# Down projections: three of eight pairs with seven products in each of three chunks, their steps alternating with half pairs, and a sixth raw buffer

## The chip, the cores and the metric

The kernel runs on one core of one Trainium2 chip. The metric is the time of one execution on the device in microseconds (us): the median of three runs, 2199.27 us before the change (2198.91 to 2200.62). The profile is of one further execution. Engines are named as the profile names them: PE is TensorE, DVE VectorE, ACT ScalarE, POOL GpSimd, SP SyncE, whose queue issues nearly all loads.

## The reference

Two transformer layers over 256 tokens of width 2048: a chunked softmax attention in the first, a stick-breaking attention in the second, each beside an attention into 256 memory tokens, and in both layers an MLP with a squared ReLU. Cut to the part that the change touches:

```
D_MODEL = 2048; SEQ = 256; D_FF = 4 * D_MODEL

def sq_relu_mlp(h, g, w_in, w_out):
    return jnp.square(jax.nn.relu(rms_norm(h, g) @ w_in)) @ w_out

for layer in range(2):
    ...
    h = h + jnp.concatenate([y_main, y_mem], axis=-1) @ w_o[layer]
    h = h + sq_relu_mlp(h, norm_mlp[layer], w_mlp_in[layer], w_mlp_out[layer])
```

`w_out` (8192 x 2048) is the down projection.

## The kernel before

All weights are float32 in HBM. Each is read once, in units of 128 x 1024 numbers (512 KB), into one of five `raw` buffers, and split into two parts that TensorE multiplies at its faster rate: `hi`, a cast by ScalarE (four buffers), and `lo = raw - hi`, a subtraction by VectorE (five buffers). A product of two split numbers takes three matmuls: hi by hi, hi by lo, lo by hi. `stream` lists the units in the order of use; `weights()` (line 235 and the lines before it are the preparing functions) hands out the next prepared unit and keeps up to four prepared ahead (`AHEAD`, 3). TensorE's instructions are kept in program order; those of VectorE, ScalarE and SyncE are put in order by a scheduler when the program is built, and each of those engines then works strictly in that order. A buffer is handed on when its last reader is done.

The MLP (`mlp`) goes through `w_in` and `w_out` in four chunks of 2048 hidden features. In each chunk an up stage (512 matmuls in the first) makes the squared activations `hid`, split in the same way (lines 1059 to 1061); then the down stage adds their product with a quarter of `w_out`. For chunks 0 to 2 the down stage is two calls of `pair_group`, one for each n, that is for 1024 of the output's columns. It goes through eight pairs j. A pair is two blocks of 128 hidden features by 1024 columns, seen as a 2 x 2 by 2 x 2 product of blocks: rows are the two halves of 128 tokens, the inner index the two feature blocks, columns the two halves of 512. There are two ways to multiply a pair:

- Directly: 8 block products, in two half pairs, one for each column half ("1" and "2"). Each half pair is one unit with one load, one cast (line 231) and one split (line 232), and takes 12 matmuls of 512 columns.
- With 7 products (`Sevenfold`, the pairs named in `SEVEN`): sums of blocks are multiplied, as in Strassen's scheme. Both sides of the pair are loaded into two raw buffers, which stay in use through four steps. Step 0 splits the left side, step 1 one block of the right side (a half-size split), step 2 subtracts twice within the raw buffers and splits the right side (lines 204, 205), step 3 adds and subtracts once more and splits the left side (lines 207, 208). The casts are line 209, the splits line 210. TensorE has 6, 3, 6 and 6 matmuls for them, 21 instead of 24. The sums of the activations, `s12` and `s34`, are made by `finish` while the up stage runs (lines 1077 to 1083).

```
if seven.step == 1:
    src, hi4, lo4 = b22, hi4[:, 0], lo4[:, 0]
elif seven.step == 2:
    nc.vector.tensor_tensor(b22, b22, b12, op=ALU.subtract)
    nc.vector.tensor_tensor(b12, b12, b11, op=ALU.subtract)
elif seven.step == 3:
    nc.vector.tensor_tensor(b11, b22, b11, op=ALU.add)
    nc.vector.tensor_tensor(b21, b21, b11, op=ALU.subtract)
nc.scalar.copy(hi4, src)
nc.vector.tensor_tensor(lo4, src, hi4.bitcast(F32), op=ALU.subtract)
```

A group adds its products in eight PSUM banks: four for the output blocks 11, 21, 12 and 22, and p1, p5, p6, p7 for the products that belong to several blocks. When a bank has its last product it is added to a buffer in SBUF (`add`, line 1019 on VectorE; in chunk 0 most are plain copies by ScalarE, line 1017): nine additions per group in chunks 1 and 2, as p1 goes to two buffers. The product sums (`extra`) are merged into the output sums by six additions per n (`merged`, line 984) after chunk 2; the scheduler puts those of the first group into the second group of that chunk. Chunk 3 has no pairs with 7 products.

Before the change the pairs with 7 products are j = 0, 3, 6 in chunk 0 and j = 2, 6 in chunks 1 and 2. A pair's four steps follow one another, and the eight pairs follow in the order of j.

Of the kernel before, what the change touches and what calls it, by code (L numbers as in the profile page):

```python
# [42 lines left out]
WARM_UP = 10  # L43


SEVEN = [(0, 3, 6), (2, 6), (2, 6), ()]


class InOrder:
# [38 lines left out]
def trunk(  # L88
# [17 lines left out]
    nc = Engines(tc)  # L106

    const = ctx.enter_context(tc.tile_pool(name="const", bufs=1))
    raws = ctx.enter_context(tc.tile_pool(name="raws", bufs=5))
    his = ctx.enter_context(tc.tile_pool(name="his", bufs=4))  # L110
    los = ctx.enter_context(tc.tile_pool(name="los", bufs=5))
    acts = ctx.enter_context(tc.tile_pool(name="acts", bufs=2))
    grp = ctx.enter_context(tc.tile_pool(name="grp", bufs=13))
    wide = ctx.enter_context(tc.tile_pool(name="wide", bufs=6))
    nar = ctx.enter_context(tc.tile_pool(name="nar", bufs=6))
    tiny = ctx.enter_context(tc.tile_pool(name="tiny", bufs=4))
    ps_mm = ctx.enter_context(tc.tile_pool(name="ps_mm", bufs=4, space=PSUM))
# [386 lines left out]
    def spread(r, scale, name):  # L504

        ps = ps_y.tile([P, 512], F32, name="spread", tag="y")
        for m in range(2):
            dg = nar.tile([P, P], F32, name="dg", tag="nar")
            nc.vector.tensor_scalar_mul(dg[:], ident[:], r[:, 2 * m : 2 * m + 1])
            mm(ps[:, m * P : (m + 1) * P], neg_ones[:], dg[:], True, True)  # L510
        rb = nar.tile([P, T], F32, name=f"rb_{name}", tag="bias", bufs=4)
        nc.vector.tensor_scalar_mul(rb[:], ps[:, :T], -1.0)
        rbs = nar.tile([P, T], F32, name=f"rbs_{name}", tag="bias", bufs=4)
        nc.vector.tensor_scalar_mul(rbs[:], rb[:], scale)
        return rb, rbs

# [130 lines left out]
        yield from soft_tail(p, [(0, T), (T, 2 * T)], rs, vm, j, y, NH + j, None, lag)  # L647

    def band_head(qt, kt_, vt, j, head, y, ready, lag):
        bias = nar.tile([P, T], F32, name="bias", tag="bias", bufs=4)  # L650
# [41 lines left out]
    def stick_head(q, kt_, vt, j, head, y, lags):  # L692
# [16 lines left out]
            out=sp[:, :N], in0=z[:, :N], scalar=0.0, in1=e[:, :N], op0=ALU.max, op1=ALU.add  # L709
        )  # L710
        strict(sp[:, :N])
        sp_hi = wide.tile([P, 512], F32R, name="sp_hi", tag="wide_r", bufs=2)
        nc.scalar.copy(sp_hi[:, :N], sp[:, :N])
        sp_lo = wide.tile([P, 512], F32R, name="sp_lo", tag="wide_r", bufs=2)
        nc.vector.tensor_tensor(
            sp_lo[:, :N], sp[:, :N], sp_hi[:, :N].bitcast(F32), op=ALU.subtract
        )
# [52 lines left out]
    def mlp_stream(l):  # L770
        for c in range(NCH):
# [169 lines left out]
    def mlp(l, xg_, sq, h, done):  # L941
# [51 lines left out]
        def pair_group(c, n, hid, factors):  # L993
# [27 lines left out]
            def tokens(kt, m):  # L1021
                return [hid[:, kt, i * T + m * P : i * T + (m + 1) * P] for i in range(2)]

            def part(unit, k2):
                return [x[:, k2 * 512 : (k2 + 1) * 512] for x in unit]

            for j in range(KT // 2):
                if j in SEVEN[c]:
                    s = [[x[:, i * P : (i + 1) * P] for x in factors[j]] for i in range(4)]
                    w = weights()  # L1030
                    add("p1", tokens(2 * j, 0), part(w, 0))
                    add("11", tokens(2 * j + 1, 0), part(w, 1))
                    w = weights()
                    add("12", s[3], part(w, 0))
                    slot()
                    w = weights()
                    add("p5", s[0], part(w, 0))
                    add("p7", s[2], part(w, 1))
                    w = weights()
                    add("p6", s[1], part(w, 0))  # L1040
                    add("21", tokens(2 * j + 1, 1), part(w, 1))
                    slot()
                    continue
                for col in "12":
                    w = weights()
                    for m in range(2):
                        for k2 in range(2):
                            add(f"{m + 1}{col}", tokens(2 * j + k2, m), part(w, k2))
                    slot()

        began = clock["slot"]
        for c in range(NCH):
# [4 lines left out]
            def finish(f, hid=hid, squares=squares, factors=factors, c=c):  # L1057
# [6 lines left out]
                if f % 2 == 0 or f // 2 not in SEVEN[c]:  # L1064
                    return

                s12 = nar.tile([P, T], F32, name="s12", tag="bias", bufs=4)
                s34 = nar.tile([P, T], F32, name="s34", tag="bias", bufs=4)
# [268 lines left out]
```

## Time and profile before

| | |
|---|---|
| Median of three runs | 2199.27 us |
| Profiled execution | 2200.56 us |
| Its span, first to last instruction | 2198.8 us |
| TensorE busy | 2185.8 us (99%), 11192 matmuls |
| VectorE busy | 1492.7 us (68%) |
| ScalarE busy | 1133.5 us (52%) |
| GpSimd busy | 322.8 us (15%) |
| Granted TensorE clock | 1.000 |
| Loads | 414.64 MB, 189 GB/s in the mean |

The page gives shares over the whole span, and stages differ, so most rows in the prediction are of a view of one stretch. A view of windows gives for each stretch its length, then busy time and number of instructions of PE, PEld (TensorE's loads of the stationary operand), DVE, ACT and POOL, then the granted clock, the DMA engines' busy share and GB/s. A timeline row is start, length, engine, line, operation, tile written and tiles read, shapes and count. A row of the chain of waits is start, length and what the end waited for in that time. A group of instructions has its count, total busy time, mean length in ns, and the engine's idle time before it with what ended that. Matmul ends are modelled: a 512-column matmul is shown with 0.39 us whether the next has begun or not, so the pace is read from starts.

### The profile page before, as it was taken

The page shows a single profiled execution, that of the slowest core. Times are in us where ns is not written, and L with a number is a line of the kernel's source. Part 1 is how long each engine was busy: PE and PEld are TensorE (multiplying, and loading weights), DVE is VectorE, ACT ScalarE, POOL GpSimd, SP SyncE. Part 2 cuts the span into 40 slices and gives each one's busy share as a digit, 9 for nine tenths or more (in the row PEclk, how much of TensorE's full clock was granted, in tenths as well). Part 3 has the DMA queues.
Part 4 walks back from the last instruction along what each step waited for, and adds up shares of the span by engine and source line. Part 5 has one row for each costly group of instructions (what it writes and reads, how often), then busy time and mean ns, then how long its engine had stood idle before and what let it go on. Part 6 is the DMA issues. An engine that isn't in the chain of part 4 may idle for free.

```text
span 2198.8 us, 30008 instructions
## 1 busy us (share of the span) xinstructions
PE 2185.8 (99%) x11192; PEld 1866.1 (85%) x11192; DVE 1492.7 (68%) x1989; ACT 1133.5 (52%) x1570; POOL 322.8 (15%) x349
## 2 busy tenths in 40 slices
PE   9999999999999999999999999999999999999999
PEld 8888888888788888888888889888878888888888
DVE  7765555677767767876676556567776777688654
ACT  7655445554555445445445447555455544444543
POOL 0010112621001001001240112362100100100100
PEclk9999999999999999999999999999999999999999
DMA  8655666655666666665666654466566567666564
GB/s 307 198 176 161 179 178 192 193 190 163 194 208 190 183 211 184 190 204 191 195 187 190 188 188 134 135 188 193 166 183 224 178 183 218 187 189 200 190 198 139
DMA packets 213313, 414.64 MB, mean 189 GB/s; under 512 B 13232, under 2 KB 144304, under 8 KB 213168
## 3 DMA queue, kind: packets, MB, share of 16 engines
q1 hardware_dynamic: 212592, 410.63, 62.2%
q10 hardware_dynamic: 576, 2.10, 0.3%
q8 instruction: 88, 1.44, 0.3%
q14 instruction: 57, 0.47, 0.1%
HBM read 410.58 MB, written 2.10 MB: 188 GB/s over the span
## 4 chain that ended last, share of the span: by engine, by line
PE 93%; DVE 3%; DMA 2%; issue 1%; ACT 1%; SPq 0%; ACTq 0%; DVEq 0%
PE acc L59 88%; DMA raw<-in_w_down 2%; PE tp L59 1%; PE yp L59 1%; DVE lo L210 1%; PE accs L59 1%; PE s L59 1%; PE z L59 1%; DVE lo L232 1%; DMA raw<-in_w_mem 1%; ACT hi L209 0%; DVE raw L207 0%; DVE raw L205 0%; DVE raw L204 0%; DVE d L1019 0%
## 5 line engine op out<-in xcount | busy, mean ns | idle before, releaser
L158 DVE TENSOR_TENSOR lo<-raw,hi 128x1024 fp32r<-128x1024 f32 (+1 forms) x524 | 643.9, 1237 | 406.4 <-ACT hi L155 286.0
L155 ACT CAST hi<-raw 128x1024 fp32r<-128x1024 f32 (+1 forms) x524 | 546.4, 1045 | 425.4 <-PE acc L59 358.2
L59 PE MATMUL acc<-hi,hid 128*128 128x512 f32 x1704 | 534.4, 390 | 0.1
L59 PE MATMUL acc<-mlpx,hi 128*128 128x512 f32 x2048 | 472.8, 390 | 0.2
L59 PEld LDWEIGHTS acc<-mlpx,hi 128*128 128x128 f32 x2048 | 381.7, 188 | 79.4 <-issue 1.7
L59 PEld LDWEIGHTS acc<-hi,hid 128*128 128x128 f32 x1704 | 319.8, 188 | 68.0 <-issue 1.3
L59 PE MATMUL acc<-lo,hid 128*128 128x512 f32 x852 | 331.9, 390 | 0.2 <-DVE lo L232 0.2
L232 DVE TENSOR_TENSOR lo<-raw,hi 128x1024 fp32r<-128x1024 f32 x192 | 231.2, 1222 | 105.7 <-ACT hi L231 104.2
L231 ACT CAST hi<-raw 128x1024 fp32r<-128x1024 f32 x192 | 198.2, 1052 | 172.1 <-PE acc L59 91.7
L1061 POOL TENSOR_TENSOR hid<-upsq,hid 128x256 fp32r<-128x256 f32 x128 | 119.4, 942 | 1109.9 <-ACT hid L1060 1109.9
L59 PEld LDWEIGHTS acc<-mlpx,lo 128*128 128x128 f32 x2048 | 250.6, 192 | 2.8
L59 PE MATMUL acc<-mlpx,lo 128*128 128x256 f32 x2048 | 252.0, 283 | 0.0
L59 PE MATMUL acc<-hi,xg 128*128 128x512 f32 x640 | 210.5, 399 | 0.0
L209 ACT CAST hi<-raw 128x1024 fp32r<-128x1024 f32 x112 | 105.8, 946 | 164.0 <-DVE raw L205 60.5
L59 PEld LDWEIGHTS acc<-lo,hid 128*128 128x128 f32 x852 | 160.0, 188 | 34.2 <-DVE lo L232 1.3
L210 DVE TENSOR_TENSOR lo<-raw,hi 128x1024 fp32r<-128x1024 f32 x112 | 121.6, 1093 | 60.6 <-ACT hi L209 60.1
L59 PEld LDWEIGHTS acc<-hi,xg 128*128 128x128 f32 x640 | 120.2, 188 | 24.6
L433 ACT COPY low<-acc 128x256 f32<-128x256 f32 x188 | 69.0, 367 | 111.2 <-PE acc L59 111.2
L59 PE MATMUL acc<-lo,xg 128*128 128x512 f32 x320 | 124.7, 390 | 0.0
L59 PE MATMUL acc<-y,hi 128*128 128x512 f32 x512 | 119.9, 391 | 0.0
L59 PEld LDWEIGHTS acc<-y,hi 128*128 128x128 f32 x512 | 95.0, 188 | 19.1
L1060 ACT CAST hid<-upsq 128x256 fp32r<-128x256 f32 x128 | 51.8, 406 | 72.1 <-DVE upsq L1059 72.0
(195 smaller groups left out, 2266.8 us busy)
## 6 DMA issues: line engine op xcount, KB each, us to landing
raw<-in_w_up SPq DMA_DIRECT2D x256, 512.0 KB, 4.3
raw<-in_w_down SPq DMA_DIRECT2D x256, 512.0 KB, 6.0
raw<-in_w_in SPq DMA_DIRECT2D x80, 512.0 KB, 3.6
raw<-in_w_o SPq DMA_DIRECT2D x64, 512.0 KB, 3.8
raw<-in_w_mem SPq DMA_DIRECT2D x28, 512.0 KB, 5.2
raw<-in_w_kv_v SPq DMA_DIRECT2D x24, 512.0 KB, 3.6
raw<-in_w_kv_k SPq DMA_DIRECT2D x24, 512.0 KB, 4.3
raw<-in_w_q SPq DMA_DIRECT2D x24, 512.0 KB, 4.2
```

Of the source, the lines that this page charges most:

```text
L59: return self._tc.keep_in_program_order(fn(*args, **kwargs))
L155: nc.scalar.copy(hi[:, :n], raw[:, :n])
L158: nc.vector.tensor_tensor(lo, raw, hi.bitcast(F32), op=ALU.subtract)
L209: nc.scalar.copy(hi4, src)
L210: nc.vector.tensor_tensor(lo4, src, hi4.bitcast(F32), op=ALU.subtract)
L231: nc.scalar.copy(hi4, turned)
L232: nc.vector.tensor_tensor(lo4, turned, hi4.bitcast(F32), op=ALU.subtract)
L433: nc.scalar.copy(low[:], bank[:, T:])
L1060: nc.scalar.copy(hid[:, f, :T], a[:])
L1061: nc.gpsimd.tensor_tensor(hid[:, f, T:], a[:], hid[:, f, :T].bitcast(F32), op=ALU.subtract)
```

## The change

`SEVEN` names three pairs, j = 0, 2 and 4, in each of chunks 0 to 2. A new function `group_order` gives the order of work in a group: step 0 of a pair, then steps 1, 2 and 3, each with one half pair of the other five pairs behind it; the half pairs of column half 1 come first, then those of half 2; the last is left for the end. The stream of loads and `pair_group` both follow it. `raws` has six buffers for five and `wide` seven for six; the tags `wide_r` (two buffers) and `qb` (three) are gone: `sp_hi` and `sp_lo` now take `wide` buffers and the q tiles of the second layer `bias` buffers, of which there are five for four.

```
-SEVEN = [(0, 3, 6), (2, 6), (2, 6), ()]
+SEVEN = [(0, 2, 4), (0, 2, 4), (0, 2, 4), ()]
+
+def group_order(sevens):
+    others = [(j, col) for col in "12" for j in range(KT // 2) if j not in sevens]
+    steps = []
+    each = len(others) // (3 * len(sevens))
+    for j in sevens:
+        steps.append((j, 0))
+        for i in (1, 2, 3):
+            steps.append((j, i))
+            steps.extend(others[:each])
+            del others[:each]
+    return steps + others
...
-    raws = ctx.enter_context(tc.tile_pool(name="raws", bufs=5))
+    raws = ctx.enter_context(tc.tile_pool(name="raws", bufs=6))
...
-    wide = ctx.enter_context(tc.tile_pool(name="wide", bufs=6))
+    wide = ctx.enter_context(tc.tile_pool(name="wide", bufs=7))
...
-        sp_hi = wide.tile([P, 512], F32R, name="sp_hi", tag="wide_r", bufs=2)
+        sp_hi = wide.tile([P, 512], F32R, name="sp_hi", tag="wide")
...
-                    for j in range(KT // 2):
+                    for j, step in group_order(SEVEN[c]):
                         sides = [unit(2 * n + i, j) for i in range(2)]
-                        if j in SEVEN[c]:
-                            stream.extend([Sevenfold(*sides)] * 4)
-                        else:
-                            stream.extend(Gathered(ap) for ap in sides)
+                        if step == 0:
+                            seven = Sevenfold(*sides)
+                        stream.append(Gathered(sides["12".index(step)]) if step in ("1", "2") else seven)
...
-            for j in range(KT // 2):
-                if j in SEVEN[c]:
...
+            for j, step in group_order(SEVEN[c]):
+                w = weights()
+                if step in ("1", "2"):
+                    for m in range(2):
+                        for k2 in range(2):
+                            add(f"{m + 1}{step}", tokens(2 * j + k2, m), part(w, k2))
                     slot()
                     continue
...
+                s = [[x[:, i * P : (i + 1) * P] for x in factors[j]] for i in range(4)]
+                pairs = [
+                    (("p1", tokens(2 * j, 0)), ("11", tokens(2 * j + 1, 0))),
+                    (("12", s[3]),),
+                    (("p5", s[0]), ("p7", s[2])),
+                    (("p6", s[1]), ("21", tokens(2 * j + 1, 1))),
+                ][step]
+                for k2, (q, a) in enumerate(pairs):
+                    add(q, a, part(w, k2))
+                if step in (1, 3):
+                    slot()
...
-        q = nar.tile([P, T], F32, name=f"qb{hd}", tag="qb", bufs=3)
+        q = nar.tile([P, T], F32, name=f"qb{hd}", tag="bias", bufs=5)
```

Two places show how rows move. The first is VectorE in chunk 0 of layer 0, at the second pair with 7 products of the first group. `raw_0` and `raw_1` are the left and the right side of that pair; a `lo` from a plain `raw` is a half pair. Before:

```order
L232 TENSOR_TENSOR lo_4987<-raw_4985,hi_4986 128x1024
L210 TENSOR_TENSOR lo_5008<-raw_0_5003,hi_5007 128x1024
L210 TENSOR_TENSOR lo_5024<-raw_1_5005,hi_5023 128x512
L204 TENSOR_TENSOR raw_1_5005<-raw_1_5005 128x4x128
L205 TENSOR_TENSOR raw_1_5005<-raw_1_5005,raw_0_5003 128x4x128
L207 TENSOR_TENSOR raw_0_5003<-raw_1_5005,raw_0_5003 128x4x128
L208 TENSOR_TENSOR raw_0_5003<-raw_0_5003 128x4x128
L210 TENSOR_TENSOR lo_5040<-raw_1_5005,hi_5039 128x1024
L210 TENSOR_TENSOR lo_5058<-raw_0_5003,hi_5057 128x1024
L232 TENSOR_TENSOR lo_5071<-raw_5069,hi_5070 128x1024
```

And now (lines 221, 222, 224 and 225 are the old 204, 205, 207 and 208; 227 is the old 210 and 249 the old 232):

```order
L227 TENSOR_TENSOR lo_4996<-raw_0_4991,hi_4995 128x1024
L227 TENSOR_TENSOR lo_5012<-raw_1_4993,hi_5011 128x512
L221 TENSOR_TENSOR raw_1_4993<-raw_1_4993 128x4x128
L222 TENSOR_TENSOR raw_1_4993<-raw_1_4993,raw_0_4991 128x4x128
L249 TENSOR_TENSOR lo_5023<-raw_5021,hi_5022 128x1024
L224 TENSOR_TENSOR raw_0_4991<-raw_1_4993,raw_0_4991 128x4x128
L225 TENSOR_TENSOR raw_0_4991<-raw_0_4991 128x4x128
L227 TENSOR_TENSOR lo_5040<-raw_1_4993,hi_5039 128x1024
L249 TENSOR_TENSOR lo_5053<-raw_5051,hi_5052 128x1024
L227 TENSOR_TENSOR lo_5061<-raw_0_4991,hi_5060 128x1024
L249 TENSOR_TENSOR lo_5080<-raw_5078,hi_5079 128x1024
```

The splits of half pairs stand between the splits of the pair, and the four operations on the raw buffers are no longer in one piece.

The second place is VectorE in chunk 2 of layer 0, where the first group ends and the second begins. `d` and `e` are the sums in SBUF: rows that read `acc` empty a PSUM bank, rows of line 984 (now 1000) are the merges. Before, the second group opens with half pairs, and its first pair with 7 products comes later:

```order
L1019 TENSOR_TENSOR d_0_4025<-acc,d_0_4025 128x512
L1019 TENSOR_TENSOR d_2_4027<-acc,d_2_4027 128x512
L232 TENSOR_TENSOR lo_8353<-raw_8351,hi_8352 128x1024
L984 TENSOR_TENSOR d_0_4025<-d_0_4025,e_0_4029 128x512
L210 TENSOR_TENSOR lo_8374<-raw_0_8369,hi_8373 128x1024
L984 TENSOR_TENSOR d_0_4025<-d_0_4025,e_1_4030 128x512
L984 TENSOR_TENSOR e_0_4029<-e_0_4029,e_2_4031 128x512
L210 TENSOR_TENSOR lo_8390<-raw_1_8371,hi_8389 128x512
```

Now the second group opens with the steps of a pair:

```order
L227 TENSOR_TENSOR lo_8347<-raw_0_8342,hi_8346 128x1024
L1035 TENSOR_TENSOR d_2_4027<-acc,d_2_4027 128x512
L227 TENSOR_TENSOR lo_8359<-raw_1_8344,hi_8358 128x512
L221 TENSOR_TENSOR raw_1_8344<-raw_1_8344 128x4x128
L249 TENSOR_TENSOR lo_8376<-raw_8374,hi_8375 128x1024
L1035 TENSOR_TENSOR d_0_4025<-acc,d_0_4025 128x512
L222 TENSOR_TENSOR raw_1_8344<-raw_1_8344,raw_0_8342 128x4x128
L1035 TENSOR_TENSOR d_2_4027<-acc,d_2_4027 128x512
L1000 TENSOR_TENSOR d_0_4025<-d_0_4025,e_0_4029 128x512
L224 TENSOR_TENSOR raw_0_8342<-raw_1_8344,raw_0_8342 128x4x128
L227 TENSOR_TENSOR lo_8403<-raw_1_8344,hi_8402 128x1024
L1000 TENSOR_TENSOR d_0_4025<-d_0_4025,e_1_4030 128x512
```

Evacuations and merges now stand between the steps of a pair, where before they stood between half pairs for the greater part.

More of the change, by code (lines that the diff above doesn't have):

```diff
@@ L510, in spread @@
             mm(ps[:, m * P : (m + 1) * P], neg_ones[:], dg[:], True, True)
-        rb = nar.tile([P, T], F32, name=f"rb_{name}", tag="bias", bufs=4)
+        rb = nar.tile([P, T], F32, name=f"rb_{name}", tag="bias", bufs=5)
         nc.vector.tensor_scalar_mul(rb[:], ps[:, :T], -1.0)
-        rbs = nar.tile([P, T], F32, name=f"rbs_{name}", tag="bias", bufs=4)
+        rbs = nar.tile([P, T], F32, name=f"rbs_{name}", tag="bias", bufs=5)
         nc.vector.tensor_scalar_mul(rbs[:], rb[:], scale)
@@ L649, in band_head @@
     def band_head(qt, kt_, vt, j, head, y, ready, lag):
-        bias = nar.tile([P, T], F32, name="bias", tag="bias", bufs=4)
+        bias = nar.tile([P, T], F32, name="bias", tag="bias", bufs=5)
         nc.sync.dma_start(
@@ L711, in stick_head @@
         strict(sp[:, :N])
-        sp_hi = wide.tile([P, 512], F32R, name="sp_hi", tag="wide_r", bufs=2)
+        sp_hi = wide.tile([P, 512], F32R, name="sp_hi", tag="wide")
         nc.scalar.copy(sp_hi[:, :N], sp[:, :N])
-        sp_lo = wide.tile([P, 512], F32R, name="sp_lo", tag="wide_r", bufs=2)
+        sp_lo = wide.tile([P, 512], F32R, name="sp_lo", tag="wide")
         nc.vector.tensor_tensor(
@@ L1025, in part @@
                 return [x[:, k2 * 512 : (k2 + 1) * 512] for x in unit]
-            for j in range(KT // 2):
-                if j in SEVEN[c]:
[L1029 to L1041, printed above, removed]
+            for j, step in group_order(SEVEN[c]):
[4 more added lines that the diff above has]
+                            add(f"{m + 1}{step}", tokens(2 * j + k2, m), part(w, k2))
                     slot()
                     continue
[L1044 to L1048, printed above, removed]
+                s = [[x[:, i * P : (i + 1) * P] for x in factors[j]] for i in range(4)]
[8 more added lines that the diff above has]
+                if step in (1, 3):
                     slot()
@@ L1065, in finish @@
                     return
-                s12 = nar.tile([P, T], F32, name="s12", tag="bias", bufs=4)
-                s34 = nar.tile([P, T], F32, name="s34", tag="bias", bufs=4)
+                s12 = nar.tile([P, T], F32, name="s12", tag="bias", bufs=5)
+                s34 = nar.tile([P, T], F32, name="s34", tag="bias", bufs=5)
                 a11, a21 = squares[f - 1][:, :P], squares[f - 1][:, P:]
```

## The prediction

> **What bounds the kernel now.** I read the page first: the engines' busy time, the granted clock and the chain that ended last.
>
> ```profile
> span 2198.8 us, 30008 instructions
> PE 2185.8 (99%) x11192; PEld 1866.1 (85%) x11192; DVE 1492.7 (68%) x1989; ACT 1133.5 (52%) x1570; POOL 322.8 (15%) x349
> ...
> PEclk9999999999999999999999999999999999999999
> ...
> PE 93%; DVE 3%; DMA 2%; issue 1%; ACT 1%; SPq 0%; ACTq 0%; DVEq 0%
> PE acc L59 88%; DMA raw<-in_w_down 2%; PE tp L59 1%; PE yp L59 1%; DVE lo L210 1%; PE accs L59 1%; PE s L59 1%; PE z L59 1%; DVE lo L232 1%; DMA raw<-in_w_mem 1%; ACT hi L209 0%; DVE raw L207 0%; DVE raw L205 0%; DVE raw L204 0%; DVE d L1019 0%
> ```
>
> TensorE carries 93% of the chain at the full clock, so a matmul that is gone is time gone. The rest of the chain is mostly the loads of w_down and the split lines L204 to L210, the lines of a pair with 7 products. All six stretches that hold such pairs are inside the change. The view of windows, cut at the first matmul of each stretch and of the up stage behind it, gives their lengths (layer 0, chunks 0, 1, 2, then layer 1); the fourth pair of numbers is VectorE's busy time.
>
> ```profile
> 529.06:618.07 89.01, 85.73 (x367) 68.07 (x366) 68.91 (x75) 50.46 (x61) 3.08 (x2) 1.00 0.67 189
> 706.89:791.66 84.77, 84.75 (x373) 69.56 (x372) 66.35 (x76) 40.86 (x43) 2.69 (x2) 1.00 0.69 196
> 880.58:966.31 85.73, 85.06 (x373) 69.49 (x372) 69.33 (x82) 40.57 (x44) 2.69 (x2) 1.00 0.68 192
> 1578.31:1667.02 88.71, 85.34 (x367) 68.13 (x366) 68.82 (x75) 50.46 (x61) 3.08 (x2) 1.00 0.67 191
> 1755.87:1840.62 84.75, 84.73 (x373) 69.55 (x372) 66.39 (x76) 40.87 (x43) 2.69 (x2) 1.00 0.70 194
> 1929.59:2015.28 85.69, 85.04 (x373) 69.46 (x372) 69.36 (x82) 40.64 (x43) 2.69 (x2) 1.00 0.69 192
> sum 518.66, PE 510.64 PEld 414.27 DVE 409.17 ACT 263.86 POOL 16.91; mean PE 85.11 PEld 69.04 DVE 68.19 ACT 43.98 POOL 2.82
> ```
>
> TensorE's timeline inside the first stretch gives the unhindered pace:
>
> ```profile
> 561.24 0.61 PE L59 MATMUL acc<-hi,hid 128*128 128x512 f32 x2
> 561.70 0.39 PE L59 MATMUL acc<-lo,hid 128*128 128x512 f32 x1
> 561.92 0.61 PE L59 MATMUL acc<-hi,hid 128*128 128x512 f32 x2
> ```
>
> Three matmuls from 561.24 to 561.92 are 0.2267 us each (0.39 is the length of one, which overlaps the next). Chunk 0 has 366 of them and needs 82.97 us, chunks 1 and 2 have 372 and need 84.33. So TensorE stands still for 6.04 and 5.74 us in chunk 0, 0.44 and 0.42 in chunk 1, 1.40 and 1.36 in chunk 2: 15.4 us in all. Busy time hides part of this, since a matmul's length reaches over a gap of 0.16 us.
>
> The chain through chunk 0 says what these gaps are:
>
> ```profile
> 534.86 8.89 DMA raw<-in_w_down
> 543.86 0.63 ACT hi L209
> ...
> 545.24 0.70 DVE raw L204
> ...
> 547.42 0.69 DVE raw L208
> 548.11 1.15 DVE lo L210
> ...
> 549.30 15.75 PE acc L59 x68
> ```
>
> A load of a right half took 8.89 us, then a cast and six VectorE operations in a row, the four subtractions and additions L204 to L208 between two splits, held TensorE back until 549.30. Why was the load so late? The DMA queue's own timeline answers, and its own waits in this chunk:
>
> ```profile
> 531.72 0.37 SPq L227 DMA_DIRECT2D raw<-in_w_down  x1
> 533.39 1.84 SPq L192 DMA_DIRECT2D raw<-in_w_down  x2
> 536.34 3.00 SPq L227 DMA_DIRECT2D raw<-in_w_down  x3
> ```
> ```profile
> SPq L227 <- DVE lo L210: 18.0, 4, 6.2
> ```
>
> Six loads leave in a clump within 8 us; then the queue waits for the split of a pair, which holds two of five raw buffers through all four steps. Loads in a clump share the 16 DMA engines, and the pair's VectorE work falls on 4.8 us of TensorE work (21 x 0.2267).
>
> **The change part by part.**
>
> *Matmuls.* There were 3, 2 and 2 pairs with 7 products in the three chunks, times two column groups and two layers: 28. Now there are 3 x 3 x 4 = 36. Each of the 8 new ones has 21 matmuls in place of 24. 8 x 3 x 0.2267 = 5.4 us off, on the path. The Trainium skill (TensorE: Matmul & The Clock Gate, Back-to-back issue gap) gives about 131 ns per matmul for a sustained stream at N=512; by that the 24 would be worth 3.1 us. The timeline above has 0.2267 in this very stage, and I keep 5.4.
>
> *VectorE's work.* The groups give the price of a pair and of a half pair:
>
> ```profile
> L232 DVE TENSOR_TENSOR lo<-raw,hi 128x1024 fp32r<-128x1024 f32 x192 | 231.2, 1222 | 105.7 <-ACT hi L231 104.2
> L210 DVE TENSOR_TENSOR lo<-raw,hi 128x1024 fp32r<-128x1024 f32 x112 | 121.6, 1093 | 60.6 <-ACT hi L209 60.1
> L231 ACT CAST hi<-raw 128x1024 fp32r<-128x1024 f32 x192 | 198.2, 1052 | 172.1 <-PE acc L59 91.7
> L208 DVE TENSOR_TENSOR raw<-raw 128x512 f32<-128x512 f32 x28 | 19.4, 692 | 0.9
> L715 DVE TENSOR_TENSOR sp_lo<-sp,sp_hi 128x384 fp32r<-128x384 f32 x12 | 6.6, 554 | 1.1 <-ACT sp_hi L713 1.1
> ```
>
> A pair costs 4 x 1.09 + 4 x 0.69 = 7.1 us (L204, L205 and L207 are the same operation as L208), two half pairs 2.4: 4.7 more per added pair, 9.3 per chunk. VectorE's busy time rises to 66.35 + 9.3 = 75.7 us in chunk 1 and 78.6 in chunk 2, of 82.97 us that TensorE needs: 91 and 95%. That is cover, but thin, so I work out the tightest place.
>
> *The alternation.* One period is now: step 0, step 1, half pair, step 2, half pair, step 3, half pair, with 6, 3, 12, 6, 12, 6, 12 matmuls: 12.9 us. Spacing of back-to-back VectorE work, from its timeline:
>
> ```profile
> 927.38 1.22 DVE L210 TENSOR_TENSOR lo<-raw,hi 128x1024 fp32r<-128x1024 f32 x1
> 928.51 0.68 DVE L984 TENSOR_TENSOR d<-d,e 128x512 f32<-128x512 f32 x1
> 929.11 0.69 DVE L984 TENSOR_TENSOR e<-e,e 128x512 f32<-128x512 f32 x1
> ```
>
> 1.13 and 0.60 us. A period needs 6 x 1.13 + 5 x 0.60 = 9.8 us: 76%. Four `hi` buffers let a cast start when the unit four places ahead is done; three units then run, 21 matmuls or 4.8 us at least (step 0, step 1, half pair), against 1.05 + 1.22 = 2.3 us for a cast and a split. Lead 2.5 us. Before, the three were steps 1 to 3, 15 matmuls or 3.4 us, with four extra subtractions (2.4 us) in the way: that is the gap at 549.30, and it goes. Late next is the end of a group in chunks 1 and 2, where nine evacuations (L1019, 128x512 as L984) come in the last eight units: these are 6 + 3 + 12 + 6 + 12 + 6 + 12 + 12 = 69 matmuls, 15.6 us, against eight splits (7 x 1.13 + 0.60), four subtractions (2.4) and nine evacuations (5.4), 16.3 us. The 0.7 us over lies inside the lead. In chunk 2 six merge additions (L984, 3.6 us) follow in the next period, whose room is 12.9 - 9.8 = 3.1: 1.2 us over in all, and the rows of the order put one split behind five of these. Both ends: 0 if the lead covers it, 1.2 if not; I take 0.4 per layer, since the lead is twice the overrun but is shared with the casts.
>
> *Loads.* With six buffers a half pair's load leaves when an earlier half pair, or the right side, is split, one at a time. The nearest need is the half pair behind step 1: its buffer comes free at step 2 of the pair ahead, and units of 6 + 3 + 12 + 6 + 12 + 6 = 45 matmuls (10.2 us) pass before its cast; the split itself takes 2.3 of that. 7.9 us are left. The loads of such weights land so:
>
> ```profile
> DMA to landing us min/median/max: 3.7/6.8/10.4
> ```
> ```profile
> raw<-in_w_down SPq DMA_DIRECT2D x256, 512.0 KB, 6.0
> ```
>
> (the tile raw in chunk 2 of layer 0, and the page's median over the program). Spread out they should be near the 3.7; at worst one is 10.4 - 7.9 = 2.5 us late, which is the size of the lead. The Trainium skill (SBUF — State Buffer, The DMA setup-cost knee) puts a transfer at about 2 us plus bytes over 436 GB/s, an estimate of 3.2 us for 512 KB; by it no load would be late with five buffers either, the sixth would be worth nothing and all 15.4 us would belong to VectorE. The 8.89 us above speaks against that. In bytes nothing is new: 16 loads per group as in chunk 0, where the windows show 189 GB/s and a DMA share of 0.67.
>
> *Work with one answer.* The third pair's factors (s12, s34) are made in the up stages of chunks 1 and 2. VectorE's timeline has one set, and the chain has TensorE without a break from the start of chunk 2's up stage on:
>
> ```profile
> 872.51 1.46 DVE L1077 TENSOR_TENSOR s<-upsq 128x128 f32<-128x128 f32 x2
> ...
> 874.64 0.76 DVE L1083 TENSOR_TENSOR s_lo<-s,s_hi 128x256 fp32r<-128x256 f32 x2
> ```
> ```profile
> 18.03 2.79 PE accs L59 x11
> ...
> 48.06 8.16 PE acc L59 x36
> ...
> 791.68 121.73 PE acc L59 x656
> ```
>
> Four more sets of 2.9 us are hidden there (11.6 us if they were not): nothing. The sixth buffer also lets loads leave earlier elsewhere. At the start one load goes ahead of loads of mem and of bias; TensorE has every row of the chain from 18.03 to 56.22, so the cost is between one load's 3.7 us and a small gain, taken as 0. The re-tagged buffers (wide, bias) leave the order in the stick-breaking stage as it was but for one sp_lo. If the shared ring made each of the 12 heads wait for one L715, it would be 12 x 0.55 = 6.6 us; taken as 0, for the ring grew by one and the q tiles keep the three places that rb and rbs leave of five.
>
> *Sum.* Gaps left: 0.4 us in each of chunks 0 and 1, as chunk 1 has now, and 0.8 in chunk 2 (0.4 and the merges' 0.4), twice: 3.2 us. Off: 15.4 - 3.2 + 5.4 = 17.6 us. The profiled execution took 2200.56 us (span 2198.8 and 1.76 around it): 2183.0. The median of the runs, 2199.27, is 1.3 below that execution: 2181.7.
>
> **The rivals.**
>
> *Three pairs cost everywhere what they cost in chunk 0.* If the gaps come from the pairs' number and not from their clumping, every chunk stands still 5.9 us: 6 x 5.9 = 35.3 against 15.4, less 5.4: 14.5 slower, 2213.8. It decides from 20.8 us of gaps in all, 3.5 per chunk. For it: the two-pair chunks have gaps of 0.4 to 1.4, the three-pair ones 6; VectorE goes to 95%. Against: the chain lays these gaps on a late load and a clump of subtractions, and both are taken apart.
>
> *VectorE is late at each group's end.* An in-order engine that waits for an evacuation's last matmul has splits queued behind it, and TensorE waits for these. If no lead is left, the overrun is paid in full: 0.7 us at each of the eight group ends of chunks 1 and 2, and the merges' 3.6 us once per layer: 5.6 + 7.2 = 12.8, less the 0.8 counted above. 2181.7 + 12.0 = 2193.7. For: it is the one place over 100%. Against: the order puts a split between most evacuations.
>
> *Loads stay late in half of the places.* Chunk 0 keeps half of its 6.04 + 5.74 = 11.8 us, 5.1 more than counted: 2186.8. For: landing times up to 10.4 us. Against: the spread issue.
>
> **How the numbers follow.** A measurement of this kernel can tell 0.2%, 4.4 us, from no change. The forecast has 0.70, the loads 0.12 (both faster), VectorE at the group ends 0.10 (half of it within 0.2%), the first rival 0.08. Faster 0.87, same 0.05, slower 0.08. The low end is all gaps gone: 2199.27 - 20.8 = 2178.5. The high end takes in the late loads and some of VectorE's case: 2190. Left out is the first rival, and most of VectorE's: 0.18 at most.
>
> **What would show it.** In the changed profile the six stretches should be 83.4 to 84 us long, 366 matmuls each; VectorE 75 to 79 us busy in chunks 1 and 2, 69 in chunk 0; the DMA queue should issue no six loads in 8 us, and w_down's loads should be near 4 to 5 us in the median (6.0 on the page now); the chain should lose most of its 2% of w_down. Wrong would be: stretches over 86 us, TensorE waiting for L227 behind an evacuation line, or new time in the stick-breaking stage.

## The result

The changed kernel takes 2180.0 us (median of four runs, 2179.85 to 2180.22) against 2199.25 us of the kernel before (2198.91 to 2200.62): ratio 0.9911, 95% interval 0.9894 to 0.9929. The forecast was 2181.7, with a range of 2178.5 to 2190.

The page of the changed kernel, its lines on the engines, the clock and the chain that ended last; line 76 is now the matmul, L225 to L227 are what L208 to L210 were, and L249 is what L232 was:

```profile
span 2178.1 us, 30022 instructions
PE 2172.7 (100%) x11168; PEld 1863.8 (86%) x11168; DVE 1535.5 (70%) x2061; ACT 1151.1 (53%) x1594; POOL 324.3 (15%) x349
...
PEclk9999999999999999999999999999999999999999
...
PE 99%; DVE 1%; ACT 0%; issue 0%; ACTq 0%
PE acc L76 94%; PE tp L76 1%; PE accs L76 1%; PE yp L76 1%; PE s L76 1%; PE z L76 1%; DVE lo L249 0%; PE cold L76 0%; DVE d L1000 0%; DVE d L1035 0%; ACT hi L248 0%; DVE raw L225 0%; DVE raw L224 0%; DVE e L1000 0%; DVE raw L222 0%
```

TensorE's share of the chain rises from 93 to 99%; the loads of w_down, 2% before, are gone from it. There are 24 matmuls fewer and 72 VectorE instructions more. The six stretches, cut as before (length, TensorE, weight loads, VectorE, ...):

```profile
528.34:611.27 82.93, 82.93 (x367) 68.69 (x366) 69.53 (x75) 50.35 (x60) 2.80 (x2) 1.00 0.73 211
700.10:783.10 83.00, 83.00 (x368) 68.70 (x367) 75.79 (x88) 44.50 (x47) 2.81 (x2) 1.00 0.72 209
871.90:955.60 83.70, 83.28 (x367) 68.62 (x366) 78.80 (x94) 44.27 (x47) 2.81 (x2) 1.00 0.70 207
1567.50:1650.40 82.90, 82.90 (x367) 68.69 (x366) 69.50 (x75) 50.35 (x60) 2.81 (x2) 1.00 0.74 211
1739.30:1822.20 82.90, 82.90 (x367) 68.69 (x366) 75.70 (x88) 44.51 (x47) 2.80 (x2) 1.00 0.73 210
1911.10:1994.70 83.60, 83.18 (x367) 68.59 (x366) 78.71 (x94) 44.29 (x47) 2.81 (x2) 1.00 0.72 207
sum 499.03, PE 498.19 PEld 412.00 DVE 448.03 ACT 278.27 POOL 16.83; mean PE 83.03 PEld 68.67 DVE 74.67 ACT 46.38 POOL 2.80
```

Each needs 366 x 0.2267 = 82.97 us. Chunks 0 and 1 take that and nothing more; chunk 2 has 0.7 us over. The six lost 518.66 - 499.03 = 19.6 us of the 20.7 by which the span shrank; the rest is 0.7 us at the start and 0.1 us in each of four up stages behind them. (The medians differ by 19.3, as the profiled execution of before was 1.3 us above its median and that of the changed kernel, 2179.85, was not.)

The chain around the boundary of chunk 2's groups shows the one gap that is left:

```profile
903.81 7.04 PE acc L76 x31
...
910.87 1.06 ACT hi L248
...
911.96 1.23 DVE lo L249
913.19 0.60 DVE d L1035
913.79 0.60 DVE raw L222
914.39 0.60 DVE d L1035
914.99 0.60 DVE d L1000
...
919.13 1.15 DVE lo L249
...
920.32 1.90 PE acc L76 x7
```

Between the splits of two half pairs VectorE has evacuations (L1035), subtractions of a pair, one split of that pair and merge additions (L1000), without a break. The chain runs through them for 9 us until the second half pair's split lets TensorE go on at 920.32: the lead has been used up.

### The profile page after: what moved, and what is told of

Same layout as the page of the kernel before. It is cut to its first block, busy times and chain, and to the rows that moved or that the text cites. A ratio compares the mean times of both kernels' runs of the same rounds, so it can differ in the third digit from the quotient of the medians.

```text
span 2178.1 us, 30022 instructions
## 1 busy us (share of the span) xinstructions
PE 2172.7 (100%) x11168; PEld 1863.8 (86%) x11168; DVE 1535.5 (70%) x2061; ACT 1151.1 (53%) x1594; POOL 324.3 (15%) x349
## 4 chain that ended last, share of the span: by engine, by line
PE 99%; DVE 1%; ACT 0%; issue 0%; ACTq 0%
PE acc L76 94%; PE tp L76 1%; PE accs L76 1%; PE yp L76 1%; PE s L76 1%; PE z L76 1%; DVE lo L249 0%; PE cold L76 0%; DVE d L1000 0%; DVE d L1035 0%; ACT hi L248 0%; DVE raw L225 0%; DVE raw L224 0%; DVE e L1000 0%; DVE raw L222 0%
## 5 line engine op out<-in xcount | busy, mean ns | idle before, releaser
L175 DVE TENSOR_TENSOR lo<-raw,hi 128x1024 fp32r<-128x1024 f32 (+1 forms) x524 | 644.6, 1237 | 391.4 <-ACT hi L172 260.4
L172 ACT CAST hi<-raw 128x1024 fp32r<-128x1024 f32 (+1 forms) x524 | 546.7, 1045 | 413.7 <-PE acc L76 350.5
L76 PE MATMUL acc<-hi,hid 128*128 128x512 f32 x1624 | 521.6, 390 | 0.0
L76 PEld LDWEIGHTS acc<-hi,hid 128*128 128x128 f32 x1624 | 304.9, 188 | 63.0
L76 PE MATMUL acc<-lo,hid 128*128 128x512 f32 x812 | 316.2, 389 | 0.8 <-DVE lo L249 0.8
L248 ACT CAST hi<-raw 128x1024 fp32r<-128x1024 f32 x176 | 185.6, 1054 | 157.8 <-PE acc L76 111.9
L249 DVE TENSOR_TENSOR lo<-raw,hi 128x1024 fp32r<-128x1024 f32 x176 | 215.0, 1221 | 74.0 <-ACT hi L248 71.5
L226 ACT CAST hi<-raw 128x1024 fp32r<-128x1024 f32 (+1 forms) x144 | 136.2, 946 | 147.0 <-PE acc L76 95.1
L227 DVE TENSOR_TENSOR lo<-raw,hi 128x1024 fp32r<-128x1024 f32 (+1 forms) x144 | 159.4, 1110 | 45.6 <-ACT hi L226 44.3
L76 PEld LDWEIGHTS acc<-lo,hid 128*128 128x128 f32 x812 | 152.5, 188 | 33.1 <-DVE lo L249 1.7
```

Source lines behind the costliest of these rows:

```text
L76: return self._tc.keep_in_program_order(fn(*args, **kwargs))
L172: nc.scalar.copy(hi[:, :n], raw[:, :n])
L175: nc.vector.tensor_tensor(lo, raw, hi.bitcast(F32), op=ALU.subtract)
L248: nc.scalar.copy(hi4, turned)
L249: nc.vector.tensor_tensor(lo4, turned, hi4.bitcast(F32), op=ALU.subtract)
```

## The experiments

The first group takes the change apart: the order (the four steps in a row, or alternating), the counts (3, 2, 2 or 3, 3, 3) and the number of raw buffers. All start from the changed kernel, so that the re-tagged buffers are the same. "Gaps" is what the six stretches take beyond their matmuls at 0.2267 us. Where a total of gaps is given, a stretch goes from its own first matmul to the first one behind it; cut so, the kernel before has 15.6 us of gaps and the changed kernel 1.5.

**Five raw buffers.**

```
-    raws = ctx.enter_context(tc.tile_pool(name="raws", bufs=6))
+    raws = ctx.enter_context(tc.tile_pool(name="raws", bufs=5))
```

> The changed kernel with five raw buffers in place of six: alternation and three pairs stay. With five, a pair's left side takes the place of the left side before it, free only at step 3, and one half pair (12 matmuls, 2.7 us) lies between that split and the cast that needs the load; a load takes 3.7 to 10 us. Theory A (both parts are needed, the sixth buffer for the loads): loads of pairs come 1 to 3 us late, the lead of 2.5 us takes most of it, some 0.3 us is left for each of 36 pairs: 2190 (2184 to 2200), TensorE gaps of 1 to 4 us in each of the six stretches. Theory B (the clump of VectorE's subtractions was the whole cause, the sixth buffer is worth nothing beyond the start): 2180.7, gaps as with six.

Measured: 2191.83 us (2189.74 to 2195.16), ratio to before 0.9964 (0.9951 to 0.9977). The windows of chunk 2 in layer 0, then chunks 0 and 2 in layer 1, and the chain through the last of them:

```profile
875.00:961.10 86.10, 84.26 (x368) 68.42 (x368) 78.87 (x94) 43.91 (x47) 2.81 (x2) 1.00 0.71 201
1572.90:1655.90 83.00, 83.00 (x368) 68.74 (x367) 69.13 (x75) 50.37 (x60) 2.81 (x2) 1.00 0.76 211
...
1917.70:2006.80 89.10, 85.20 (x368) 68.14 (x367) 78.93 (x94) 44.04 (x47) 2.81 (x2) 1.00 0.70 194
```
```profile
1951.33 8.94 DMA raw<-in_w_down
1960.36 1.06 ACT hi L248
1961.44 1.23 DVE lo L249
...
1969.78 5.89 DMA raw<-in_w_down
```

With three pairs in every chunk the buffer decides: loads of 8.94 and 5.89 us stand in the chain again. The time is that of theory A, its picture is not: the 12.7 us of gaps are not spread over the pairs, one chunk 0 has none and the last chunk 2 has 6.

**The old order and counts, six buffers.** `group_order` gives a pair's four steps in a row and the pairs in the order of j, and `SEVEN` is that of before:

```
+    for j in range(KT // 2):
+        steps.extend([(j, i) for i in range(4)] if j in sevens else [(j, "1"), (j, "2")])
```

> The changed kernel's buffers (six raw ones and the new tags) with the order and the counts of before: four steps of a pair in a row, 3, 2 and 2 pairs. Theory A (both parts are needed): the loads' share of the 15.4 us of gaps goes, VectorE's clump stays: about half, 2191 (2188 to 2195). Theory B (VectorE's clump is all): 2198.5, gaps of 5 to 6 us in chunk 0 as before, only the start's 0.7 us gone. Theory C (late loads are all, the sixth buffer is the cure): 2184, gaps gone but for 1.4 us.

Measured: 2192.02 us (2191.70 to 2192.72), ratio 0.9964 (0.9950 to 0.9979). Chunks 0 and 1 of layer 0, and the chain through chunk 0 (the line of the matmul is L70 here, L218 to L221 the last additions and the split of a pair):

```profile
528.30:613.20 84.90, 83.99 (x367) 68.39 (x367) 69.23 (x75) 50.66 (x61) 3.33 (x2) 1.00 0.71 198
702.00:786.70 84.70, 84.68 (x373) 69.58 (x371) 66.37 (x76) 40.89 (x43) 2.68 (x2) 1.00 0.71 195
```
```profile
529.14 0.49 DVE raw L219
...
529.75 1.23 DVE lo L221
...
531.02 1.65 PE acc L70 x6
```

The gaps of chunk 0 fall from 5.9 to 1.9 us, and no load is left in its chain; the 0.4 and 1.4 us of chunks 1 and 2 stay as they were. So the buffer alone takes 8.1 of the 15.6 us away. Of the 7.5 that are left, some 5.6 are waits for a pair's split by VectorE; 1.8 lie at the group ends of chunks 1 and 2, where the trace shows no engine that TensorE waits for. Theories B and C both fall. That 8 us go with the buffer doesn't make them the loads' own: alternation takes them away without it, as the run with the old counts and five buffers shows below.

**Three pairs in every chunk in the old order, six buffers.** Only `group_order` is undone.

> The changed kernel with the order of before: three pairs in every chunk and six raw buffers stay, the four steps of a pair stand in a row again. Theory A: 5.4 us of matmuls and 0.7 us at the start off, and each of the six stretches has the half of chunk 0's 5.9 us that the buffer doesn't cure: 2193.2 + 18 - 15.4 = 2196 (2190 to 2202). Theory B (VectorE's clump is all): 6 x 5.9 = 35 us of gaps, 2213. Theory C (the sixth buffer is the cure, the order does nothing): 2180.

Measured: 2196.70 us (2196.03 to 2198.04), ratio 0.9983 (0.9974 to 0.9993): 1.4, 2.9 and 4.5 us of gaps in chunks 0, 1 and 2 (means of the two layers), 17.7 in all. The total is theory A's, but the gaps grow with VectorE's load from chunk to chunk, where it had put 3 us in each. Beside the sixth buffer, alternation is worth 17.7 - 1.5 = 16 us with three pairs.

**Three pairs in the old order, five buffers.** As the last, with five raw buffers: the first rival of the prediction, made real.

> Three pairs in every chunk with the order of before and five raw buffers: the counts of the changed kernel without alternation and without the sixth buffer. Theory A (late loads and VectorE's clump add up, and both are what alternation and the sixth buffer take away): the 5.9 us of chunk 0 before in every stretch, and in chunks 1 and 2 also the 1.5 and 3.1 us that they had over chunk 0 with six buffers: 6 x 5.9 + 2 x 4.6 = 44.6 us of gaps, 2199.3 + 44.6 - 15.4 - 5.4 = 2223 (2213 to 2230). The first rival of the prediction (as many pairs, as many gaps) gives 2213.8. Theory C (the pairs' number does not matter once their clumps are short): as old_order_three, 2197.

Measured: 2217.86 us (2217.57 to 2219.34), ratio 1.0077 (1.0061 to 1.0092). Layer 0 (chunks 0, 1, 2):

```profile
529.20:616.00 86.80, 86.00 (x368) 67.88 (x367) 69.42 (x75) 50.57 (x61) 2.54 (x2) 1.00 0.75 204
704.80:794.90 90.10, 86.09 (x368) 68.06 (x367) 76.35 (x88) 44.34 (x48) 2.55 (x2) 1.00 0.73 196
883.60:975.80 92.20, 86.99 (x368) 67.85 (x367) 79.65 (x94) 44.06 (x48) 2.54 (x2) 1.00 0.70 194
```

38 us of gaps, where the rival had 35.3: the counts alone make the kernel slower. Its total was nearly right, in part by luck, for it had put 5.9 us in every stretch and they are 3.8 in chunk 0, 6 to 7 in chunk 1 and 8 to 9 in chunk 2. What it lacked was that alternation and the buffer take the cause away.

**Alternation with the old counts**, `SEVEN = [(0, 3, 6), (2, 6), (2, 6), ()]`, six buffers.

> The changed kernel with the counts of before (3, 2 and 2 pairs): alternation and six buffers stay, the third pair in chunks 1 and 2 goes. Theories A and B: gaps as in the changed kernel, 24 matmuls more at 0.2267 us: 2180.0 + 5.4 = 2185.4, and VectorE's 9.3 us less per chunk change nothing. Rival (VectorE at the group ends limits the changed kernel): chunk 2's gap of 0.69 us goes too, 2184.1, and chunk 1 needs no more than 84.4 us.

Measured: 2184.33 us (2183.57 to 2185.02), ratio 0.9927 (0.9912 to 0.9941). No stretch has a gap, chunk 2 neither: with two pairs VectorE has room for the merges. The rival's 2184.1 is met, so the 0.7 us of the changed kernel's chunk 2 are VectorE's.

**The same with five buffers.**

> Alternation with the counts of before (3, 2 and 2 pairs) and five raw buffers. Theory A (with five buffers a pair's left side is loaded only when the pair before it is done; with two pairs, two half pairs or 5.4 us lie between, with three pairs one): gaps of about 0.5 us in chunk 0, none in chunks 1 and 2: 2184.3 + 1 = 2185.5. Rival (five buffers make loads late wherever steps and half pairs alternate): half of what they cost with three pairs, 6 us, 2190.

Measured: 2184.74 us (2183.66 to 2186.48), ratio 0.9928 (0.9913 to 0.9942). Chunks 0 and 2 of layer 0:

```profile
528.77:612.50 83.73, 83.42 (x368) 68.52 (x367) 69.09 (x75) 50.16 (x60) 2.81 (x2) 1.00 0.72 208
874.47:958.79 84.32, 84.32 (x374) 69.84 (x372) 70.84 (x82) 41.17 (x43) 3.23 (x2) 1.00 0.71 207
```

One gap of 0.8 us, in chunk 0 of layer 0, none elsewhere: theory A holds, the rival falls. The gaps in all six stretches, in us, side by side:

| | five buffers | six buffers |
|---|---|---|
| 3, 2 and 2 pairs, steps in a row | 15.6 (before) | 7.5 |
| 3, 2 and 2 pairs, alternating | 0.8 | 0.0 |
| three pairs, steps in a row | 38.3 | 17.7 |
| three pairs, alternating | 12.7 | 1.5 (the changed kernel) |

So the two causes are not two separate amounts. With the counts of before, alternation alone removes nearly all the gaps, those behind late loads among them, and beside it the sixth buffer is worth nothing that shows. It is worth 11 us where three pairs alternate in every chunk, most of it in chunk 2; chunk 0, which has three pairs in both kernels with five buffers, loses 1 us at most.

The second group tries the limit that is left, VectorE.

**The merges on GpSimd.**

```
-                nc.vector.tensor_tensor(dst, dst, src, op=ALU.add)
+                nc.gpsimd.tensor_tensor(dst, dst, src, op=ALU.add)
```

> The changed kernel with the twelve merge additions of chunk 2 in each layer on GpSimd in place of VectorE. Theory A (the last 0.69 us in chunk 2 are VectorE's merges between the splits): chunk 2 shrinks from 83.7 to 83.0 us in both layers, 2178.6. Rival (GpSimd's additions slow VectorE down beside them, or come too late for what reads the sums): no gain, 2180.0 or more, and VectorE's splits in chunk 2 longer than 1.22 us.

Measured: 2184.96 us (2184.60 to 2186.19), 5 us more than the changed kernel, ratio to before 0.9925 (0.9909 to 0.9942). Chunk 2 grew by 3.5 and 2.4 us. Both layers have a wait of 2.4 us for a split; in layer 0 the granted clock was 0.5 in the 3.41 us from 923.59, just behind it, which accounts for some 1.6 us of the 3.5, while in layer 1 it stayed at 1.00. VectorE's timeline and GpSimd's at the boundary:

```profile
914.12 0.68 DVE L222 TENSOR_TENSOR raw<-raw,raw 128x512 f32<-128x512 f32 x1
...
918.67 1.77 DVE L225 TENSOR_TENSOR raw<-raw 128x512 f32<-128x512 f32 x1
920.37 2.28 DVE L249 TENSOR_TENSOR lo<-raw,hi 128x1024 fp32r<-128x1024 f32 x1
```
```profile
917.63 2.27 POOL L1000 TENSOR_TENSOR e<-e,e 128x512 f32<-128x512 f32 x1
919.98 1.59 POOL L1000 TENSOR_TENSOR d<-d,e 128x512 f32<-128x512 f32 x1
```

An addition of the pair takes 1.77 us in place of 0.69, a split 2.28 in place of 1.22, while GpSimd adds beside them. The two evacuations (L1035) that began under a GpSimd addition kept their 0.68 us; they read one of their inputs from PSUM. Theory A falls and the rival holds: this moves VectorE's work to an engine that slows VectorE down. The Trainium skill (SBUF — State Buffer, SBUF: two separate sides) calls the port pair that the two engines share an exclusive lock, held for a whole instruction, which VectorE's operations with two inputs from SBUF want as well. The trace agrees: L225, 0.69 us alone, begins at 918.67 under a GpSimd addition that runs to 919.90, and ends 0.5 us behind it.

**Four pairs in every chunk.** Two half pairs behind a pair's steps 1 and 2; nine wide buffers for the factors, and four lo buffers to make room:

```
-SEVEN = [(0, 2, 4), (0, 2, 4), (0, 2, 4), ()]
+SEVEN = [(0, 2, 4, 6)] * 3 + [()]
-    each = len(others) // (3 * len(sevens))
+    halves = (1, 1, 1) if len(sevens) == 3 else (1, 1, 0)
-        for i in (1, 2, 3):
+        for i, each in zip((1, 2, 3), halves):
-    los = ctx.enter_context(tc.tile_pool(name="los", bufs=5))
+    los = ctx.enter_context(tc.tile_pool(name="los", bufs=4))
-    wide = ctx.enter_context(tc.tile_pool(name="wide", bufs=7))
+    wide = ctx.enter_context(tc.tile_pool(name="wide", bufs=9))
```

> Four pairs in every chunk, alternating with two half pairs each (behind steps 1 and 2), nine wide buffers for the fourth pair's factors and four lo buffers. TensorE needs 360 x 0.2267 = 81.6 us in a stretch. VectorE's busy time would be 69.5, 75.8 and 78.8 us plus 9.4: 79, 85 and 88 us, of which overlap takes some 0.09 us per operation. Theory A (VectorE's cover ends here): chunk 0 gap-free, gaps of some 2 us in chunk 1 and 4 to 6 us in chunk 2: 8.2 us of matmuls off, 12 to 14 us of gaps more: 2184 (2179 to 2190). Rival (the alternation covers a fourth pair as well): 2173.

Measured: 2187.32 us (2186.68 to 2187.62), ratio 0.9936 (0.9921 to 0.9951). Layer 0:

```profile
528.46:610.08 81.62, 81.62 (x362) 67.53 (x361) 76.47 (x87) 52.88 (x64) 7.69 (x2) 1.00 0.74 205
699.00:782.95 83.95, 82.49 (x362) 67.37 (x360) 81.82 (x97) 47.49 (x51) 7.69 (x2) 1.00 0.72 201
871.80:958.28 86.48, 84.23 (x362) 68.45 (x361) 85.17 (x103) 47.22 (x51) 7.70 (x2) 0.98 0.70 195
```

Chunk 0 takes its 81.6 us; chunks 1 and 2 have gaps of 2.3 and 4.9, with VectorE busy for 97 and 98% of the stretch. The 0.98 of chunk 2 is a granted clock of 0.5 for 3.41 us behind two waits, some 1.6 us of its gaps; in layer 1 the clock was full and the gaps 4.5 us. Theory A's gaps are met; the time is 3 us above its figure. In the profile 2.1 us more than in the changed kernel lie outside the stretches, in the last up stages and the stick-breaking part.

**Four pairs, with sums and merges on GpSimd.** As the last, the merges as above, and:

```
-                        nc.vector.tensor_tensor(dst, banks[q][:], dst, op=ALU.add)
+                        for u in range(2):
+                            x = slice(u * T, (u + 1) * T)
+                            t = nar.tile([P, T], F32, name="ev", tag="nar")
+                            nc.scalar.copy(t[:], banks[q][:, x])
+                            nc.gpsimd.tensor_tensor(dst[:, x], t[:], dst[:, x], op=ALU.add)
```

> As four_pairs, and the evacuations of chunks 1 and 2 that add into a sum are done by ScalarE (two copies of 128x256) and GpSimd (two additions), and the merges by GpSimd. This takes 18 x 0.69 = 12 us and in chunk 2 another 4 us off VectorE. Theory A (VectorE is what limits four pairs): no gaps, 2180.0 - 8.2 - 1.4 = 2170.4 (2169 to 2173). Rival (ScalarE's copies stand ahead of casts, or GpSimd slows VectorE down): gaps of 2 us or more in chunks 1 and 2, 2176 or more.

Measured: 2212.39 us (2212.31 to 2212.72), ratio 1.0051 (1.0036 to 1.0066). A group of chunk 2 in layer 0, and the chain at the boundary of chunk 1's groups (L1039 is the addition by GpSimd, L1038 the copy by ScalarE):

```profile
L227 DVE TENSOR_TENSOR lo<-raw,hi 128x1024 fp32r<-128x1024 f32 x23 | 32.9, 1445 | 1.1 <-ACT hi L226 1.0
```
```profile
741.00 4.11 POOL e L1039 x4
...
746.80 0.38 ACT ev L1038
747.18 0.95 ACT hi L226
```

VectorE is busy 89.2 us in chunk 2, more than with the evacuations in its own queue, as a split takes 1445 ns in the mean. The gaps are 6.5 and 11.5 us in chunks 1 and 2. Both halves of the rival are seen: GpSimd's additions slow VectorE down, and ScalarE's copies wait for these additions with the casts behind them. Some 7 of the 36 us of gaps lie in five stretches of 3.41 us with a granted clock of 0.5 behind such waits. Theory A falls; how much of it each half costs was not taken apart.

The last group looks for a better version; the changed kernel ran beside it on the same chip.

> The changed kernel as it is, for the runs that are compared with it on one chip: 2180 as before, at most 2 us more where this chip runs the kernel of before slower as well.

Measured: 2180.12 us (2179.69 to 2180.50).

**The merges kept in program order**, so that they fall behind the second group:

```
-                nc.vector.tensor_tensor(dst, dst, src, op=ALU.add)
+                tc.keep_in_program_order(nc.vector.tensor_tensor(dst, dst, src, op=ALU.add))
```

> The changed kernel with the merge additions kept in program order, so that VectorE has none of them at the boundary of chunk 2's groups and all twelve in the up stage of chunk 3 (88.8 us, of which VectorE is busy for some 62). Theory A (the last 0.69 us in chunk 2 are these additions between the splits): chunk 2 takes 83.0 in place of 83.7 us in both layers, 1.4 us less than the changed kernel beside it. Rival (it is the evacuations at the boundary that use up the lead, whatever follows): chunk 2 stays at 83.7 or gains less than half.

Measured: 2180.08 us (2179.57 to 2180.52): no gain. Chunk 2 of layer 0, and the chain of layer 1 behind chunk 2:

```profile
872.36:955.33 82.97, 82.97 (x368) 68.70 (x367) 75.75 (x88) 44.50 (x47) 2.81 (x2) 1.00 0.73 210
```
```profile
2029.46 0.68 DVE e L1000
...
2031.36 0.61 DVE d L1000
...
2032.02 0.55 PE tp L76 x3
```

Theory A is right where it looked: the 0.7 us go in both layers (83.7 to 82.97). But in layer 1 the merged sums are transposed in the next up stage, and TensorE now waits for the last merge at 2031.97: that up stage grows by 1.1 us. The start was 0.4 us longer in this execution. A stall was moved, not removed.

**The same, with four pairs in chunk 0 alone** (`SEVEN = [(0, 2, 4, 6), (0, 2, 4), (0, 2, 4), ()]`, the halves and buffers of four_pairs).

> merges_ordered with four pairs in chunk 0 alone, where VectorE has only the evacuations of two banks (busy 69.5 us of 83.0); nine wide and four lo buffers, as in four_pairs. Theory A: chunk 0 has 360 matmuls and no gap, 81.6 in place of 83.0 us in both layers, 2.7 us less; with the merges 4.1 us less than the changed kernel beside it. Rival (the fourth pair's factors, made in the up stage of chunk 0, or the four lo buffers cost as much): no more than 1.4 us less.

Measured: 2178.54 us (2177.92 to 2178.93), below every run of the changed kernel beside it, which began at 2179.69. Chunk 0 takes 81.63 us in both layers, 1.33 less each, and chunk 2 0.7 less each, as theory A has it: 4.1 us. Of this 1.9 are given back in layer 1's up stage with the transposes and 0.5 in the stick-breaking part, which four_pairs shows too (0.5). The time fell by 1.6 us, near the rival's 1.4 and far from theory A's 4.1. Whether four lo or nine wide buffers cost the latter was not tried.

## Why the prediction was right

- **Matmuls, 5.4 us:** as priced. 366 matmuls stand in every stretch, at 82.97 us where nothing waits. The 131 ns per matmul of the Trainium skill (TensorE: Matmul & The Clock Gate, Back-to-back issue gap) were not seen here.
- **VectorE's work:** 75.7 and 78.6 us were expected in chunks 1 and 2, 75.8 and 78.8 were measured; chunk 0 has 69.5 (68.9 before).
- **The lead of 2.5 us through alternation:** it holds everywhere but at the boundary of chunk 2. The 0.4 us that were left over for each of chunks 0 and 1 were too much: the chain through chunk 0 is one piece of TensorE's work. Gaps left: 1.5 us measured, 3.2 forecast; and before had 15.6 us of them, where the sum has 15.4. Against the profiled execution, 2183.0 forecast and 2179.85 measured, the 3.1 us are these 1.7 and 0.2, the start's 0.7 and 0.4 in the up stages. That the median came only 1.7 below the forecast is in part luck: the 1.3 us by which before's execution was above its median have no counterpart here.
- **The end of the groups:** the 0.7 us by which VectorE's work exceeds the room are taken by the lead in chunk 1, as said; the merges behind them cost chunk 2 its 0.7 us. The forecast had 0.8 for chunk 2, but made up otherwise: 0.4 for the merges and 0.4 that every chunk was to keep. That the merges are the cost is shown by the ordered merges, where chunk 2 has no gap, and the old counts agree.
- **Loads:** the clump went. Before, 19 loads of w_down began a stretch of 8 us with six of them; now none does. The queue's timeline in the first chunk, and its longest wait there, now for a half pair's split, one load at a time:

```profile
529.68 0.37 SPq L209 DMA_DIRECT2D raw<-in_w_down  x1
531.41 4.12 SPq L244 DMA_DIRECT2D raw<-in_w_down  x3
536.64 5.24 SPq L209 DMA_DIRECT2D raw<-in_w_down  x2
```
```profile
SPq L209 <- DVE lo L249: 34.4, 8, 10.7
```
```profile
raw<-in_w_down SPq DMA_DIRECT2D x256, 512.0 KB, 5.6
```

 The step that failed is the landing time: 4 to 5 us in the median were expected, 5.6 were measured (6.0 before). For the loads issued within the six stretches the medians were 6.8 to 7.9 us before and are 5.5 to 5.9 now; spreading the loads did not bring them near 3.7 us. It didn't matter, as the slack of 7.9 us covers most of them: the longest in chunk 2 of layer 0 was 6.8 us, 10.4 before. With five buffers and three pairs 11 us of gaps come back.
- **The start:** taken as nothing, it gave 0.7 us in the profile. The buffer doesn't decide it: other kernels here with six buffers have a stretch from the first matmul to the first up stage of 437.7 to 439.2 us, the changed kernel 437.9, the kernel before 438.7. The chains point to when the first loads land: that of before begins with loads of w_mem of 5.29 and 6.68 us, that of the changed kernel has none there.
- **Factors of the third pair and re-tagged buffers:** nothing, as said. The up stages between are 88.8 us as before or 0.1 less, and the stick-breaking part agrees within 0.1 us.
- **The rivals:** the first is real where order and buffer stay as before (2217.9 against its 2213.8). The second and third did not happen; their nearest relatives are the 0.7 us of chunk 2, and the changed kernel with five buffers.

## What to carry to other kernels

A stall at the hand-over from a preparing engine to TensorE can have two parts, when the data comes and how much other work stands between two hand-overs. Undo each of them alone as well as both: here the buffer alone was worth half of the stall, alternation alone nearly all of it. The queue's waits for a pair's split before the change fit this: work in a clump also holds the buffers that the next loads need. The gain in matmuls could be had only with both. VectorE, 91% busy over chunk 1, still covered everything once its work alternated with TensorE's; look at the boundaries, where extra work lands, for what is left. And whether work can be moved to an idle engine depends on what that engine shares with the busy one.

## What the runs showed that was not expected

- GpSimd's additions beside VectorE's stretch VectorE's operations with two inputs from 0.69 to 1.77 us and from 1.22 to 2.28 us. The merges beside chunk 2 cost it 5.9 us in the two layers, 1.6 of them at half the clock. With the evacuations as well, by way of ScalarE's copies, it was 25 us against the same kernel without (2212.4 to 2187.3).
- Behind some of the longest waits of TensorE the granted clock was 0.5 for 3.41 us. It did not follow every wait of a length: of two waits of 2.4 us with the merges on GpSimd one had it.
- The kernels whose gaps hang on loads seem to spread more from run to run: 2189.7 to 2195.2 with five buffers, 2198.2 to 2204.2 before on one chip, against 2179.7 to 2180.5 for the changed kernel (2199.1 to 2202.1 of before beside it) and 2191.7 to 2192.7 for the old order with six buffers, whose gaps are mostly VectorE's. These are 4 to 15 runs each, and with alternation, the old counts and five buffers the runs spread by 2.8 us with hardly a gap. So it is not shown that the loads are the cause.
